# Inverse norms by VectorE alone, spread by products with the identity, and conv operands loaded three to a product

## The chip, the cores and the metric

The kernel runs on one core of one Trainium2 chip. The metric is the device time of one execution in microseconds (us). Engines are named as the profile names them: PE is TensorE (PEld its weight loads), DVE is VectorE, ACT is ScalarE, POOL is GpSimd, SP is SyncE, whose queue here issues nearly all DMA transfers. L217 means line 217 of the kernel.

## What is computed

One layer of a streaming encoder over 1056 tokens (1024 of a prompt, 32 of a sample), model width 1024, all in float32: a sliding-window attention and a gated short convolution side by side, then attention to 256 memory tokens, then an MLP, each behind an RMS norm. Cut to what matters:

```python
def rms_norm(x, g):
    y = x * rsqrt(mean(x * x, axis=-1, keepdims=True) + 1e-6)
    return y * g

h = rms_norm(x, g_mix)
q, k, v, ch, cb, cc, ga, gb = split(h @ w_in)
a = window_attention(q, k, v) @ w_attn_out
conv = causal_depthwise_conv3(cc * ch)
bo = (cb * conv) @ w_conv_out
x = x + (sigmoid(ga) * a + sigmoid(gb) * bo) @ w_mix_out
hc = rms_norm(x, g_cross)
x = x + memory_attention(hc @ w_cq, mem_k, mem_v) @ w_co
hm = rms_norm(x, g_mlp)
x = x + square(relu(hm @ w_up)) @ w_down
y = rms_norm(x, g_final)
```

The keys and values of the memory tokens come from a further RMS norm of the memory input.

## The kernel before

**Layout.** Activations lie transposed: features on the 128 partitions (eight groups of 128, f = 0 to 7), tokens along the free dimension. The tokens are cut into three chunks of 384, 384 and 288 columns (CH). Every float32 product is made of three passes in fp32r: each operand x is split into a rounded part hi (written by ACT) and the rest lo = x - hi (written by DVE), and hi*hi, hi*lo and lo*hi are summed. So a product of a 128-feature output group is 24 matmuls with 24 weights of 128 by 128 (gemm, L183 to L185; the MLP's are at L851 to L853 and L1586 to L1588). A weight of 128 by 1024 is fetched by SP (L145), split by ACT (L125) and DVE (L126), two or three ahead of its use.

**Order.** The work is written as a list of items; a planner with a timeline of its own then orders the instructions of each engine and hands out buffers from pools. Where an instruction is wrapped in pin, it stays in program order with the other pinned ones of its engine. Each engine runs its own instructions in that order, and a waiting instruction holds back all behind it. Scratch tiles named "ct" come from one ring of six buffers (NCT, function tmp). Accumulators in PSUM ("acc") are three until the last stage and six in it.

**Norms.** Most products are made of x times the gain, and their result is multiplied by the inverse norm of its token; for that, and where an operand is normed ahead (L820, L1212), all 128 partitions need the inverse norms as a row, R. chunk_stats does this in two steps. stats_col: squares are summed over feature groups, then per block of 128 tokens a product with a column of ones gives the sum of squares as a column of 128 tokens (pq, L214); DVE scales it and adds the epsilon (L216), ACT takes the square root (L217), DVE the reciprocal (L218) and one Newton step (L219 to L221), which leaves up to three columns in rcol. stats_row: per block the identity is scaled by the column, as hi on ACT (L229) and lo on DVE (L230), into two ct tiles; two products with a matrix of ones (L231, L232) sum each over the partitions and so leave the inverse norms along the free dimension in all partitions (pr), which ACT copies to R (L242) or, for the memory, to mr (L404). stats_col runs 13 times: three times at the start (norm_x), once for the memory, twice for each chunk around the attention to the memory, three times for the final norm. stats_row runs 12 times; the last chunk to be finished, chunk 1, needs columns alone, as it is turned by transposes and leaves token by token (final_last, L1654).

ACT holds one table of functions at a time. Square root, exponential and sigmoid sit in different ones, and a load is seen in the trace (ACT_TABLE_LOAD) where the next function needs another. At the start norm_x takes a dummy square root (L282), so that the first real one finds its table.

**From the gates to the mix.** The gate pairs end the projections of the first stage. close_gates (L865) then lists the conv operands of chunks 1 and 2, eight tiles each, in `wanted`, and starts the first two. A call pump(n) first splits the tiles that the call before had loaded (ACT L781, DVE L782, both pinned) and then issues n more loads (L786), each into a ct tile. Next comes trunk(0): eight conv output products of chunk 0 (do_conv_out, one for each f), then its eight mix products (do_mix). A conv output product loads m1, the gated attention part, into a ct tile (L1026), multiplies the accumulator by the gate into another (DVE, L1030), adds m1 (POOL, L1031, or DVE for the last f) and splits the sum for the mix. Beside its eight conv output products runs the pump, two loads to a product. Small loads of the memory's keys and values (L1056, L1065), with splits of their own (L1068, L1069), are placed in the same stretch by the planner. The mix of chunk 0 needs all eight sums. Trunks 1 and 2 follow, with the attention of the chunk before to the memory set between their products by hand (beside, cross_steps); do_co (L1183 to L1187) ends that attention, do_mix adds x (L1045), and normed_split (L1212 to L1216) prepares the MLP's operands.

The lines behind the pump beside trunk(0):

```python
left = beside([], trunk(0), [(i, lambda: pump(2)) for i in range(NF)])
item(lambda: pump(0))
```

Of the kernel before, what the change touches and what calls it, by code (L numbers as in the profile page):

```python
# [9 lines left out]

F32 = mybir.dt.float32
F32R = mybir.dt.float32r
AF = mybir.ActivationFunctionType
ALU = mybir.AluOpType
AX = mybir.AxisListType
# [3 lines left out]
P = 128  # L19
# [4 lines left out]
NF = 8  # L24
# [14 lines left out]
def hybrid_step(ctx: ExitStack, tc: tile.TileContext, io):  # L39
    nc = tc.nc  # L40
    act, dve, pool_e, pe, sp = nc.scalar, nc.vector, nc.gpsimd, nc.tensor, nc.sync
# [3 lines left out]
    def nm(s):  # L45
        uid[0] += 1
        return f"{s}_{uid[0]}"
# [11 lines left out]
    misc = ctx.enter_context(tc.tile_pool(name="misc", bufs=1))  # L59
# [6 lines left out]
    prm = misc.tile([P, NPARAM], F32, name="prm")  # L66
    ident = misc.tile([P, P], F32, name="ident")
    ones = misc.tile([P, 1], F32, name="ones")
    ones_r = misc.tile([P, P], F32R, name="ones_r")
    nsink = misc.tile([P, 20], F32, name="nsink")  # L70

    def col(j):
# [28 lines left out]
    def tmp(n, dt=F32):  # L101
        return tp.tile([P, n], dt, tag="ct", bufs=NCT, name=nm("ct"))

    def slot(pool, tag, n, dt=F32R, bufs=None):
        return pool.tile([P, n], dt, tag=tag, bufs=bufs, name=nm(tag))
# [8 lines left out]
    def item(fn, *keys):  # L114
        plan.append((fn, keys))
        worder.extend(keys)
# [31 lines left out]
    def issue_w():  # L148
# [3 lines left out]
        key = worder[wpos[0]]  # L152
        hi = wp.tile([P, 1024], F32R, tag="wh", name=nm("wh"))
        lo = wp.tile([P, 1024], F32R, tag="wl", name=nm("wl"))
        if kept.get(key) is not None:
# [52 lines left out]
    def stats_col(accs, blocks, rcol):  # L208

        nb = len(blocks)  # L210
        pq = ps.tile([P, nb], F32, tag="pt", bufs=2, name=nm("pq"))
        for j, b in enumerate(blocks):
            for i, acc in enumerate(accs):
                pe.matmul(pq[:, j : j + 1], acc[:, b : b + P], ones, start=(i == 0), stop=(i == len(accs) - 1))  # L214
        v, s, y, t = (misc.tile([P, nb], F32, tag=x, bufs=2, name=nm(x)) for x in ("st_v", "st_s", "st_y", "st_t"))
        dve.tensor_scalar(v, pq, 1.0 / D, EPS, op0=ALU.mult, op1=ALU.add)  # L216
        act.activation(s, v, AF.Sqrt)  # L217
        dve.reciprocal(y, s)  # L218
        dve.tensor_mul(t, v, y)  # L219
        dve.scalar_tensor_tensor(t, t, -0.5, y, op0=ALU.mult, op1=ALU.mult)  # L220
        dve.scalar_tensor_tensor(rcol, t, 1.5, y, op0=ALU.add, op1=ALU.mult)  # L221

    def stats_row(blocks, n, rcol):

        pr = ps.tile([P, n], F32, tag="pt", bufs=2, name=nm("pr"))
        dh, dl = tmp(n, F32R), tmp(n, F32R)
        for j, b in enumerate(blocks):
            s, r, eye = slice(j * P, b + P), rcol[:, j : j + 1], ident[:, j * P - b :]
            act.mul(dh[:, s], eye, r)  # L229
            dve.scalar_tensor_tensor(dl[:, s], eye, r, dh[:, s].bitcast(F32), op0=ALU.mult, op1=ALU.subtract)  # L230
        pe.matmul(pr, ones_r, dh, start=True, stop=False)  # L231
        pe.matmul(pr, ones_r, dl, start=False, stop=True)  # L232
        return pr

    def chunk_col(c):
# [12 lines left out]
    def square_acc(x, f, c, on_pool=False):  # L248
# [7 lines left out]
        else:  # L256
            act.activation(sq, x, AF.Square)  # L257
        if f:
# [18 lines left out]

    def norm_x():
        pool_e.memset(ones, 1.0)
        act.copy(ones_r, ones.to_broadcast([P, P]))  # L280
        warm = misc.tile([P, 1], F32, name="warm")
        act.activation(warm, ones, AF.Sqrt)  # L282
        make_identity(nc, ident)
        raws = []

        def load_x():
            for c, (o, n) in enumerate(CH):
                raw = raw_tile()[:, : NF * n].rearrange("p (f t) -> p f t", f=NF)
                for h in range(4):
                    sp.dma_start(raw[:, 2 * h : 2 * h + 2], io[f"x{c}"][:, 2 * h : 2 * h + 2])  # L290
                    if c == h == 0:
                        sp.dma_start(prm, io["params"])
                        fetch_w()
                if c == 0:
                    fetch_w()
                    fetch_w()
                raws.append(raw)

        def parts(c, fs, pinned=lambda x: x):
            for f in fs:  # L300
                xg[c][f] = (slot(xpool, f"X{c}", CH[c][1]), slot(xpool, f"X{c}", CH[c][1]))
                scaled_split(*xg[c][f], raws[c][:, f], G_MIX + f, pinned)

        def squares(c):
            n = CH[c][1]
            acc = st.tile([P, n], F32, tag="sum", bufs=2, name=nm("sum"))
            for f in range(NF):
                sq = st.tile([P, n], F32, tag="sq", bufs=2, name=nm("sq")) if f else acc
                (pin if c else lambda x: x)(act.activation(sq, raws[c][:, f], AF.Square))
                if f:  # L310
                    dve.tensor_add(acc, acc, sq)
            accs[c] = [acc]

        with tc.manual_schedule(engines={mybir.EngineType.SP}):
            load_x()
        with tc.manual_schedule(engines={mybir.EngineType.Activation, mybir.EngineType.DVE}):
            parts(0, range(2))
            issue_w()
            parts(0, range(2, NF))
            issue_w()  # L320
            issue_w()
            squares(0)
        wk, wv = ready[0][1], (ready[1][1], ready[2][1])
        kt = at_tile([P, NT], F32, "kt")
        ktt[0] = kt
        vs3 = {}

        def scaled(c):

            o, n = CH[c]  # L330
            chunk_row(c)
            k = kt[:, o : o + n]
            pool_e.tensor_tensor(k, k, R[c], op=ALU.mult)
            for j in range(3):
                v_scale(vs3[c, j], c, j)

        for c, (o, n) in enumerate(CH):
            a = acc_tile([P, n])
            gemm(a, wk, xg[c])
            act.copy(kt[:, o : o + n], a)  # L340
            if c < 2:
                parts(c + 1, range(NF), pin)
            vs3[c, 0] = v_block(wv, c, 0)
            if c:
                scaled(c - 1)
            chunk_col(c)
            vs3[c, 1] = v_block(wv, c, 1)
            vs3[c, 2] = v_block(wv, c, 2)
            if c < 2:
                squares(c + 1)  # L350
            if c == 1:
                mem_load_x()
        for key in start_keys:
            next_w(key)

        def end():
            scaled(2)
            sp.dma_start(io["o_k"][0], kt[:, 896:])
            v = tmp(256)
            sp.dma_start(v, io["cache_v"])  # L360
            vtile(v)
            dve.tensor_scalar_mul(nsink, prm[:, SINK0 : SINK0 + 20], -1.0)

        start_end.extend([(0, end), (2, mem_parts)])
# [10 lines left out]
    def mem_parts():  # L375
        mx = mact.pop()
        his, los = (raw_tile(F32R)[:, : NF * 256].rearrange("p (f t) -> p f t", f=NF) for _ in range(2))
        for f in range(NF):
# [399 lines left out]
    def pump(n):  # L778
        for into, at, t, get in coming:
            hi, lo = into[at] = (get(), get())  # L780
            pin(act.copy(hi, t))  # L781
            pin(dve.tensor_sub(lo, t, hi.bitcast(F32)))  # L782
        coming.clear()
        for into, at, src, cols, get in wanted[:n]:
            t = cols() if callable(cols) else tmp(cols)
            sp.dma_start(t, src)  # L786
            coming.append((into, at, t, get))
        del wanted[:n]
# [684 lines left out]
    def beside(steps, fillers, late=()):  # L1473
        for i, filler in enumerate(fillers):
            item(*filler)
            for x in [x for at, x in late if at == i]:
                item(lambda x=x: x())
            if steps:
                kind, what = steps.pop(0)
                for x in what:  # L1480
                    if kind == "items":
                        item(*x)
                    else:
                        item(lambda x=x: x())
        return steps

    def trunk(c):
        return [(do_conv_out(c, f), ("w_conv_out", f)) for f in range(NF)] + [
            (do_mix(c, f), ("w_mix", f)) for f in range(NF)
        ]  # L1490
# [2 lines left out]
    for name, n in (("w_conv_out", NF), ("w_mix", NF), ("w_cq", 2), ("w_co", 2), ("w_up", NF)):  # L1493
        kept.update(((name, j), None) for j in range(1, n, 2))

    left = beside([], trunk(0), [(i, lambda: pump(2)) for i in range(NF)])
    item(lambda: pump(0))
    left = beside(cross_steps(0), trunk(1))

    normed = lambda c, at: [(at + f, lambda f=f: normed_split(c, f)) for f in range(NF)]  # L1500
    left = beside(left + cross_steps(1), trunk(2), normed(0, 6))
    left = beside(left + cross_steps(2), up0(0) + up0(1), normed(1, 0))
# [337 lines left out]
```

## Time and profile before

| | |
|---|---|
| median of three runs | 1791.7 us |
| lowest and highest run | 1789.65 and 1793.85 us |
| profiled execution, span | 1791.7 us |
| busy: PE, DVE, ACT, POOL | 1754.1, 1173.1, 799.6, 594.2 us |
| moved by DMA | 331.5 MB, mean 185 GB/s |
| mean granted clock of TensorE | 0.994 |

The profile is of one execution on the chip. A row of a group gives line, engine, operation, output and inputs, shapes, count, busy time and mean duration of one, and the idle time of the engine just before them with what ended it. A row in order of time gives start, duration and the instruction, with the wait before it in brackets. Matmuls are pipelined: their durations overlap, and what one costs in a stream is the distance from its start to the next start. A stretch gives the busy time of each engine, the TensorE clock that was granted (1.00 is full speed), the share of time that the DMA engines were busy and what they moved.

### The profile page before, as it was taken

Reading aid. Unit: us, or ns where it says so; the run is one execution under the profiler, and the core shown is the slowest. Engines: PE = TensorE matmul, PEld = TensorE weight load, DVE = VectorE, ACT = ScalarE, POOL = GpSimd, SP = SyncE. Lnnn points to the kernel's source line nnn. Section 1 sums busy time; section 2 is a strip of 40 time slices with the busy share of each in tenths; the row PEclk is TensorE's granted clock in tenths of the full one; section 3 lists DMA queues with packets and bytes.
Section 4 is the critical chain, followed back from the end, with each engine's and each line's share of the span. In section 5 each row is a group of like instructions: output and inputs, shape, how many; then the busy total and the mean of one; then the engine's idle time right before and its main releaser. Section 6 shows DMA issues by size and latency. Waiting matters only on the chain. (4 is left out here: it accounts for less than half of the span.)

```text
span 1791.7 us, 30247 instructions
## 1 busy us (share of the span) xinstructions
PE 1754.1 (98%) x11110; PEld 1732.5 (97%) x11110; DVE 1173.1 (65%) x2165; ACT 799.6 (45%) x1566; POOL 594.2 (33%) x681
## 2 busy tenths in 40 slices
PE   8999999999999999999999989999999999999997
PEld 8999999999999999999999989999999999999997
DVE  6776767868666646546566777767566676436763
ACT  8643534435345334334565745632222343324453
POOL 0013146553453444511224142386554300100111
PEclk9999999999999999999999999999999999999999
DMA  5232234344346888758765657754333487446673
GB/s 181 98 116 92 87 104 153 118 142 144 137 151 239 286 281 282 270 196 274 261 208 201 229 187 252 254 180 148 131 127 137 150 291 246 144 131 214 198 234 125
DMA packets 183858, 331.50 MB, mean 185 GB/s; under 512 B 18768, under 2 KB 139376, under 8 KB 183584
## 3 DMA queue, kind: packets, MB, share of 16 engines
q1 hardware_dynamic: 169936, 281.18, 46.7%
q0 software_dynamic: 13776, 48.41, 7.6%
q8 instruction: 87, 1.43, 0.3%
q14 instruction: 59, 0.48, 0.1%
HBM read 242.99 MB, written 86.52 MB: 184 GB/s over the span
## 5 line engine op out<-in xcount | busy, mean ns | idle before, releaser
L126 DVE TENSOR_TENSOR wl<-wr,wh 128x1024 fp32r<-128x1024 f32 x225 | 300.9, 1337 | 178.6 <-ACT wh L125 175.8
L125 ACT CAST wh<-wr 128x1024 fp32r<-128x1024 f32 x225 | 236.8, 1052 | 401.1 <-PE acc L1587 103.1
L183 PE MATMUL acc<-X,wh 128*128 128x384 f32 (+1 forms) x864 | 282.2, 327 | 8.2 <-ACT wh L125 8.2
L184 PE MATMUL acc<-X,wh 128*128 128x384 f32 (+1 forms) x864 | 279.4, 323 | 0.0
L185 PE MATMUL acc<-X,wl 128*128 128x384 f32 (+1 forms) x864 | 278.9, 323 | 0.3 <-DVE wl L126 0.3
L183 PE MATMUL acc<-Y,wh 128*128 128x384 f32 (+1 forms) x624 | 201.9, 325 | 0.8 <-DVE ct L1242 0.3
L185 PE MATMUL acc<-Y,wl 128*128 128x384 f32 (+1 forms) x624 | 202.1, 324 | 0.0
L184 PE MATMUL acc<-Y,wh 128*128 128x384 f32 (+1 forms) x624 | 201.7, 324 | 0.0
L259 POOL TENSOR_TENSOR xacc<-xacc,ct 128x384 f32<-128x384 f32 (+1 forms) x62 | 75.4, 1218 | 339.8 <-ACT ct L257 334.2
L183 PEld LDWEIGHTS acc<-X,wh 128*128 128x128 f32 x864 | 163.2, 189 | 8.8 <-ACT wh L125 8.2
L184 PEld LDWEIGHTS acc<-X,wh 128*128 128x128 f32 x864 | 163.5, 189 | 0.6
L185 PEld LDWEIGHTS acc<-X,wl 128*128 128x128 f32 x864 | 163.1, 189 | 0.8 <-DVE wl L126 0.8
L183 PEld LDWEIGHTS acc<-Y,wh 128*128 128x128 f32 x624 | 117.4, 189 | 1.8 <-DVE ct L1089 0.6
L185 PEld LDWEIGHTS acc<-Y,wl 128*128 128x128 f32 x624 | 117.8, 189 | 0.0
L184 PEld LDWEIGHTS acc<-Y,wh 128*128 128x128 f32 x624 | 117.7, 189 | 0.0
L1586 PE MATMUL acc<-Y,wh 128*128 128x384 f32 (+1 forms) x352 | 112.7, 322 | 1.1 <-DVE lt L1378 0.7
L1587 PE MATMUL acc<-Y,wh 128*128 128x384 f32 (+1 forms) x352 | 113.1, 321 | 0.0
L1588 PE MATMUL acc<-Y,wl 128*128 128x384 f32 (+1 forms) x352 | 112.8, 321 | 0.0
L125 ACT CAST PTh<-pt 128x512 fp32r<-128x512 f32 (+3 forms) x94 | 46.2, 517 | 115.8 <-PE pt L572 107.8
L707 POOL TENSOR_TENSOR xacc<-xacc 128x256 f32<-128x256 f32 x92 | 83.7, 909 | 4.9
L851 PE MATMUL acc<-Y,wh 128*128 128x384 f32 x248 | 83.1, 336 | 1.8 <-ACT wh L125 1.8
L1244 POOL TENSOR_TENSOR ct<-ct 128x288 f32<-128x288 f32 (+1 forms) x48 | 45.2, 943 | 116.7 <-DVE ct L1240 45.7
(360 smaller groups left out, 4759.5 us busy)
## 6 DMA issues: line engine op xcount, KB each, us to landing
wr<-in_w_in SPq DMA_DIRECT2D x53, 512.0 KB, 3.5
wr<-in_w_up SPq DMA_DIRECT2D x48, 512.0 KB, 4.0
wr<-in_w_down SPq DMA_DIRECT2D x32, 512.0 KB, 4.0
wr<-wsum_d SPq DMA_DIRECT2D x32, 512.0 KB, 3.9
wl<-wl_d SPq DMA_DIRECT2D x28, 512.0 KB, 4.6
wr<-in_w_conv_out SPq DMA_DIRECT2D x24, 512.0 KB, 4.4
wr<-in_w_mix SPq DMA_DIRECT2D x24, 512.0 KB, 4.4
ct<-b_d SPq DMA_DIRECT2D x48, 192.0 KB, 4.1
```

Source lines behind the costliest of these rows:

```text
L125: act.copy(hi, src)
L126: dve.tensor_sub(lo, src, hi.bitcast(F32))
L183: pe.matmul(out, wh[:, a], hi, start=(k == 0), stop=False)
L184: pe.matmul(out, wh[:, a], lo, start=False, stop=False)
L185: pe.matmul(out, wl[:, a], hi, start=False, stop=(k == len(acts) - 1))
L259: pool_e.tensor_tensor(acc, acc, sq, op=ALU.add)
L707: pin(pool_e.tensor_tensor(t[:, to], t[:, x], t[:, y], op=ALU.add))
L851: pe.matmul(acc, wh[:, a], hi, start=(start and k == 0), stop=False, skip_group_check=True)
L1244: pool_e.tensor_tensor(h, t, t, op=ALU.mult)
L1586: pe.matmul(a, wh[:, s], hi, start=(start and k == 0), stop=False, skip_group_check=True)
L1587: pe.matmul(a, wh[:, s], lo, start=False, stop=False, skip_group_check=True)
L1588: pe.matmul(a, wl[:, s], hi, start=False, stop=(stop and k == len(acts) - 1), skip_group_check=True)
```

## The change

Three things. The inverse norm no longer goes through ACT: its first guess comes from integer operations on the bits of the value (a shift to the right by one, then a constant minus the result), followed by three Newton steps in place of one, all on DVE. The column is spread over rows by products: the column is rounded to fp32r as rh, the rest is rl, and for each block of 128 tokens the column, repeated 128 times by its access pattern, is the weight and the identity in fp32r the moving operand; so no scaled identity and no ct tile is needed. The dummy square root at the start and the matrix of ones go, a copy of the identity in fp32r comes. And the pump beside the conv output products of chunk 0 loads three tiles to a product for products 0 to 4, and splits the last of them at product 5.

```diff
-    ones_r = misc.tile([P, P], F32R, name="ones_r")
+    ident_r = misc.tile([P, P], F32R, name="ident_r")
...
-        v, s, y, t = (misc.tile([P, nb], F32, tag=x, bufs=2, name=nm(x)) for x in ("st_v", "st_s", "st_y", "st_t"))
+        v, y, t = (misc.tile([P, nb], F32, tag=x, bufs=2, name=nm(x)) for x in ("st_v", "st_y", "st_t"))
         dve.tensor_scalar(v, pq, 1.0 / D, EPS, op0=ALU.mult, op1=ALU.add)
-        act.activation(s, v, AF.Sqrt)
-        dve.reciprocal(y, s)
-        dve.tensor_mul(t, v, y)
-        dve.scalar_tensor_tensor(t, t, -0.5, y, op0=ALU.mult, op1=ALU.mult)
-        dve.scalar_tensor_tensor(rcol, t, 1.5, y, op0=ALU.add, op1=ALU.mult)
+        dve.tensor_single_scalar(t.bitcast(I32), v.bitcast(I32), 1, op=ALU.arith_shift_right)
+        dve.tensor_scalar(y.bitcast(I32), t.bitcast(I32), -1, 0x5F3759DF, op0=ALU.mult, op1=ALU.add)
+        for to in (y, y, rcol):
+            dve.tensor_mul(t, v, y)
+            dve.scalar_tensor_tensor(t, t, -0.5, y, op0=ALU.mult, op1=ALU.mult)
+            dve.scalar_tensor_tensor(to, t, 1.5, y, op0=ALU.add, op1=ALU.mult)
...
         pr = ps.tile([P, n], F32, tag="pt", bufs=2, name=nm("pr"))
-        dh, dl = tmp(n, F32R), tmp(n, F32R)
+        rh, rl = (misc.tile([P, len(blocks)], F32R, tag=x, bufs=2, name=nm(x)) for x in ("st_h", "st_l"))
+        dve.tensor_copy(rh, rcol)
+        dve.tensor_sub(rl, rcol, rh.bitcast(F32))
         for j, b in enumerate(blocks):
-            s, r, eye = slice(j * P, b + P), rcol[:, j : j + 1], ident[:, j * P - b :]
-            act.mul(dh[:, s], eye, r)
-            dve.scalar_tensor_tensor(dl[:, s], eye, r, dh[:, s].bitcast(F32), op0=ALU.mult, op1=ALU.subtract)
-        pe.matmul(pr, ones_r, dh, start=True, stop=False)
-        pe.matmul(pr, ones_r, dl, start=False, stop=True)
+            s, eye = slice(j * P, b + P), ident_r[:, j * P - b :]
+            for r in (rh, rl):
+                pe.matmul(pr[:, s], r[:, j : j + 1].to_broadcast([P, P]), eye, start=(r is rh), stop=(r is rl))
         return pr
...
         pool_e.memset(ones, 1.0)
-        act.copy(ones_r, ones.to_broadcast([P, P]))
-        warm = misc.tile([P, 1], F32, name="warm")
-        act.activation(warm, ones, AF.Sqrt)
         make_identity(nc, ident)
+        act.copy(ident_r, ident)
...
-    left = beside([], trunk(0), [(i, lambda: pump(2)) for i in range(NF)])
-    item(lambda: pump(0))
+    left = beside([], trunk(0), [(i, lambda i=i: pump(3 if i < 5 else 0)) for i in range(6)])
```

More of the change, by code (lines that the diff above doesn't have):

```diff
@@ L12 @@
 F32R = mybir.dt.float32r
+I32 = mybir.dt.int32
 AF = mybir.ActivationFunctionType
```

## The prediction

> **What bounds the kernel now.** I read the page first, then the busy time in stretches of 20 us, then TensorE's own waits. The page:
>
> ```profile
> span 1791.7 us, 30247 instructions
> PE 1754.1 (98%) x11110; PEld 1732.5 (97%) x11110; DVE 1173.1 (65%) x2165; ACT 799.6 (45%) x1566; POOL 594.2 (33%) x681
> ```
>
> TensorE (PE) is busy for 98% of the span, and no other engine is near that. So a microsecond of products added is, as a rule, a microsecond of time, and a microsecond taken from ScalarE (ACT) or VectorE (DVE) is worth something only where PE stood idle for it. The idle time is 1791.7 - 1754.1 = 37.6 us. The stretches say where (columns: stretch, length, busy time of PE, PEld, DVE, ACT, POOL, then granted clock, DMA share, GB/s):
>
> ```profile
> 680.00:700.00 20.00, 17.09 (x85) 16.30 (x85) 13.14 (x16) 7.05 (x13) 10.10 (x14) 0.83 0.78 264
> 820.00:840.00 20.00, 19.55 (x112) 19.06 (x110) 13.75 (x22) 10.72 (x19) 3.65 (x4) 1.00 0.84 283
> 840.00:860.00 20.00, 18.07 (x99) 17.12 (x100) 15.01 (x26) 11.73 (x22) 4.14 (x3) 1.00 0.75 251
> 1020.00:1040.00 20.00, 15.26 (x97) 13.67 (x96) 16.46 (x28) 12.45 (x23) 6.76 (x6) 0.95 0.73 253
> 1040.00:1060.00 20.00, 18.10 (x103) 17.10 (x103) 15.53 (x22) 10.24 (x18) 13.31 (x13) 0.88 0.49 159
> 1740.00:1760.00 20.00, 19.00 (x106) 17.93 (x106) 10.61 (x15) 11.77 (x20) 4.54 (x4) 1.00 0.64 207
> 1780.00:1800.00 20.00, 3.27 (x31) 3.03 (x29) 2.89 (x8) 3.19 (x6) 0.00 (x0) 0.79 0.22 80
> sum 1800.00, PE 1754.10 PEld 1732.51 DVE 1173.12 ACT 799.59 POOL 594.22; mean PE 19.49 PEld 19.25 DVE 13.03 ACT 8.88 POOL 6.60
> ```
>
> The end, after the last product, holds 11.7 - 3.3 = 8.4 us of it. The largest hole inside is 1020 to 1060 (4.7 + 1.9 = 6.6 us), where attention to the memory of chunk 1 runs beside the mix of chunk 2; then 680 to 700 (2.9 us) and 820 to 860 (0.45 + 1.93 = 2.4 us), the step from the conv output products to the mix of chunk 0. TensorE's waits and the start:
>
> ```profile
> PE acc L183 <- ACT wh L125: 9.8, 2, 8.2
> PE acc L1183 <- DVE Gb L1045: 3.9, 4, 1.5
> 4.19 1.12 ACT L262 ACTIVATE X<-raw,prm 128x384 fp32r<-128x384 f32 x2 [0.35 <-DMA prm<-in_params]
> 7.07 1.05 ACT L125 CAST wh<-wr 128x1024 fp32r<-128x1024 f32 x1 [1.75 <-DMA wr<-in_w_in]
> ```
>
> The 8.2 us are the start. There ACT waits for the parameters at 4.19 and the first weight at 7.07, so a table load and a dummy square root less ahead of 4.19, and a copy of the identity in their place, change nothing: 0. No wait of PE names a line of the norm (L216 to L242).
>
> **The change part by part.** The profiled execution spans 1791.7 us, which is also the median of the runs (1791.7, between 1789.65 and 1793.85), so the sum is made against 1791.7.
>
> *Row products.* Twelve calls spread inverse norms over rows. Each now issues two products of 384, 288 or 256 columns; afterwards six of up to 128 columns (four for the memory), each with a weight of its own.
>
> ```profile
> L231 PEld LDWEIGHTS pr<-ct,ones_r x12: 187/188/192, 36.1 to 1732.2; 128*128 128x128 f32 x12
> L231 PE MATMUL pr<-ct,ones_r x12: 279/331/338, 36.2 to 1732.3; 128*128 128x384 f32 x7, 128*128 128x288 f32 x4, 128*128 128x256 f32 x1
> 95.42 0.27 PE L546 MATMUL sc<-KSh,QA 128*128 128x128 f32 x1
> 95.98 0.28 PE L547 MATMUL sc<-KSl,QA 128*128 128x128 f32 x1
> 1732.35 0.33 PE L231 MATMUL pr<-ct,ones_r 128*128 128x384 f32 x1
> 1732.52 0.34 PE L1587 MATMUL acc<-Y,wh 128*128 128x384 f32 x1
> 785.83 0.29 PE L185 MATMUL pa<-X,wl 128*128 128x288 f32 x1
> 785.96 0.29 PE L183 MATMUL pa<-X,wh 128*128 128x288 f32 x1
> ```
>
> Durations overlap, so the price is from start to start: 0.17 us for 384 columns, 0.13 for 288. For 128 columns in fp32r, 95.42 and 95.98 are the first and the last of six in a row, five steps: 0.56 / 5 = 0.112 us. They don't cost a third of 384. A row of 384 goes from 2 x 0.17 = 0.34 to 6 x 0.112 = 0.67, plus 0.33; of 288 from 0.26 to 0.67, plus 0.41 (its last block has 32 columns, taken at the same price); the memory's from 0.26 (the 288 row) to 0.45, plus 0.19. Sum 7 x 0.33 + 4 x 0.41 + 0.19 = **4.1 us**, on the bounding engine. No row shows a weight that is one column read 128 times. Below: 0, if 128 columns cost a third of 0.17, as 6 x 0.057 = 0.34. Above: the load's 0.188 us uncovered, 6 x 0.188 = 1.13, so 7 x 0.79 + 4 x 0.87 + (0.75 - 0.26) = 9.5. I take 4.1, the row of the same shape.
>
> The Trainium skill's page "TensorE: Matmul & The Clock Gate" (section on LDWEIGHTS) prices a load by its 128 columns at 107 ns, which the 0.112 agrees with; its section "Back-to-back issue gap" gives 81 ns for 128 columns in a stream of such pairs. By that the rows would cost 7 x 0.15 + 4 x 0.23 + 0.06 = 2.0, an estimate from that page, and the whole would come out some 2 us lower.
>
> *ACT and DVE.* Removed: 35 scalings by the identity on each engine, 13 square roots and their table loads, of which ACT holds:
>
> ```profile
> L217 ACT ACT_TABLE_LOAD x4 | 5.1, 1283 | 0.1
> L1125 ACT ACT_TABLE_LOAD x3 | 3.8, 1283 | 0.1
> L229 ACT ACTIVATE ct<-ident,rc 128x128 fp32r<-128x128 f32 (+1 forms) x33 | 10.6, 385 | 1.6 <-DVE rc L221 1.6
> L230 DVE SCALAR_TENSOR_TENSOR ct<-ident,rc,ct x33: 246/346/918, 33.0 to 1732.6; 128x128 fp32r<-128x128 f32 x29, 128x32 fp32r<-128x32 f32 x4
> ```
>
> That is about 10.6 + 5.1 + most of 3.8 = 19 us less on ACT. DVE loses 33 x 0.35 = 12 us and 13 reciprocals and gains, by call, two integer operations and six of Newton (13 x 8 x 0.16 = 17 us) and two small copies a row (24 x 0.16 = 4): about +7. Both lie under PE's products, so 0; without that cover DVE's 7 us would count. Two "ct" buffers of six are no longer held for a row, worth something only where PE waits behind that ring (the second rival).
>
> *The end.* Here nothing hides the norm:
>
> ```profile
> 1782.92 0.16 DVE L216 TENSOR_SCALAR st_v<-pq 128x3 f32<-128x3 f32 x1 [2.92 <-PE pq L214]
> 1783.12 0.20 ACT L217 ACTIVATE st_s<-st_v 128x3 f32<-128x3 f32 x1 [1.91 <-DVE st_v L216]
> 1783.76 0.16 DVE L220 SCALAR_TENSOR_TENSOR st_t<-st_t,st_y 128x3 f32<-128x3 f32 x1
> 1783.96 0.16 DVE L221 SCALAR_TENSOR_TENSOR rc<-st_t,st_y 128x3 f32<-128x3 f32 x1
> ```
>
> Dependent operations on DVE start 0.20 apart. Now the last one starts 1.04 after the first; afterwards it is the eleventh after it, 11 x 0.20 = 2.2. So **+1.2 us**, and the outputs and their stores follow that much later. An integer operation isn't shown; at half or twice 0.20 for the two the term is 1.0 to 1.6.
>
> *Norm of chunk 0 near the end.* Between 1725.94 and 1733.95 its chain stands among other DVE work:
>
> ```profile
> 1725.94 0.15 DVE L216 TENSOR_SCALAR st_v<-pq 128x3 f32<-128x3 f32 x1
> 1733.95 0.48 ACT L242 COPY R<-pr 128x384 f32<-128x384 f32 x1 [0.83 <-PE pr L232]
> ```
>
> 8.0 us. The trip to ACT and the scalings go, nine more DVE operations come, each behind whatever stands there. Outputs of chunk 0 wait for it, and behind these on SP the last operand loads, for which PE is idle 1.0 us at 1740 to 1760. Between -1.0 (that idle gone) and +1.8 (nine at 0.20, none hidden); I take 0.
>
> *Conv operands, three to a product.* After the gates' own two, 14 loads remain; two to a product they end at product 6, three to a product at product 4, and the last splits (L781, L782) come at product 5 rather than after 6. The loads on SP move ahead of weight loads and of m1 (L1026). Now:
>
> ```profile
> 806.97 0.56 DVE L1030 TENSOR_TENSOR ct<-acc,Ga 128x384 f32<-128x384 f32 x1 [1.21 <-PE acc L185]
> 843.51 0.55 DVE L1030 TENSOR_TENSOR ct<-acc,Gb 128x384 f32<-128x384 f32 x1
> 819.59 1.01 POOL L1031 TENSOR_TENSOR ct<-ct,ct 128x384 f32<-128x384 f32 x1 [4.42 <-DVE mkl L126]
> 820.63 0.32 SPq L1026 DMA_DIRECT2D ct<-m_d  x1
> 840.14 0.44 PE L183 MATMUL acc<-M,wh 128*128 128x384 f32 x1 [0.58 <-DVE ct L1030]
> 852.50 0.44 PE L183 MATMUL acc<-M,wh 128*128 128x384 f32 x1 [1.66 <-ACT wh L125]
> 851.09 0.41 ACT L1068 CAST mv<-mvr 128x256 fp32r<-128x256 f32 x1 [1.61 <-DMA mvr<-in_cmem_v]
> ```
>
> DVE takes up a conv product every (843.51 - 806.97) / 7 = 5.2 us, where PE needs 24 x 0.17 = 4.1: a load of m1 is issued when POOL's add of the product before has freed its buffer. DVE ends some 7 us late and PE pays 0.58, then 1.66 behind a load for the memory in ACT's queue. With no operand loads in the last three products that stretch of DMA is lighter. At best all 2.4 us idle of 820 to 860 go; at worst the first five products get slower (third rival). I take **-1.0**: the 0.58 and a quarter of the rest, as the loop through POOL remains.
>
> Sum: 4.1 + 1.2 + 0 - 1.0 = +4.3, so **1796.0 us**, with its own range 1792 to 1800.
>
> **The rivals.**
> *One: the small products hide their weight loads* and the rows cost nothing: 1791.7 + 1.2 - 1.0 = 1791.9. For it, 128 x 0.17 / 384 = 0.057; against it, the run at 0.112.
> *Two, on the other side: faster.* Lighter ACT and two more free buffers let the adds of L1045 come in time and the hole at 1020 to 1060 closes. Its price is 6.6 us idle and what the clock lost there, 20 x (0.05 + 0.12) = 3.4: 1796.0 - 10.0 = 1786.0. It decides once L1183 no longer waits for L1045. For it, the seven table loads of L217 and L1125 fall between 887 and 1154 us, and most go; against it, DVE is the fuller engine there (16.5 of 20) and gains work.
> *Three: three loads starve the ring of six.* A load more is 0.196 MB at 283 GB/s = 0.7 us a product, so 5.9 us against 4.1; after five DVE is 9 us late, more than the two spare accumulators cover (2 x 4.1). PE then waits about 2 us, and an idle time of this kind has cost the clock:
>
> ```profile
> 687.21 0.69 PE L851 MATMUL acc<-X,wh 128*128 128x384 f32 x1 [2.91 <-ACT wh L125]
> ```
>
> In its stretch the clock fell to 0.83, 20 x 0.17 = 3.4 us. Together 1796.0 + 1.0 + 2 + 3.4 = 1802.4.
> *Four: loads of the repeated column don't overlap*: 9.5 for 4.1, 1801.4.
>
> **How the numbers follow.** Forecast 0.44, rivals one 0.12, two 0.24, three 0.14, four 0.06. A measurement of this kernel can tell about 0.2%, 3.6 us, from no change: the bounds are 1788.1 and 1795.3. Faster: rival two but for 0.02, 0.22. Within: one 0.12, 0.02 of two, and 0.16 of the forecast (its range from 1792 up to 1795.3): 0.30. Slower: the remaining 0.28, three and four: 0.48. The range runs from 1786.5 to 1802, leaving out half of two and half of three.
>
> **What would show it.** Row products at 0.11 from start to start, 70 in place of 24; eleven DVE steps of 0.20 at the end; no table load after 900; L1030 every 5 us or so and less idle at 840 to 860. Wrong, if the row products take 0.06 or 0.19, or if idle time between 800 and 1180 moves by more than 4 us either way, since the planner orders everything anew.

## The result and the profile after

| | before | after |
|---|---|---|
| median, four runs each, side by side | 1792.8 us | 1806.3 us |
| lowest and highest run | 1789.65 and 1795.52 us | 1802.1 and 1809.16 us |
| profiled execution, span | 1791.7 us | 1803.8 us |

The changed kernel is slower: the ratio is 1.0081, 95% interval 1.0057 to 1.0106, or 14.5 us with 10 to 19. The forecast was 1796.0 us, and its range ended at 1802. The page of the changed kernel, its first line and its busy times:

```profile
span 1803.8 us, 30353 instructions
PE 1757.3 (97%) x11156; PEld 1737.1 (96%) x11156; DVE 1182.3 (66%) x2245; ACT 776.0 (43%) x1509; POOL 594.7 (33%) x681
```

PE executes 46 more products, ACT is 24 us lighter and DVE 9 us heavier; 19 and 7 were forecast. PE's busy time grew by 3.2 us and its idle time by 8.9 (from 37.6 to 46.5). The same stretches of 20 us say where the idle time is (columns as before):

```profile
680.00:700.00 20.00, 18.25 (x99) 17.49 (x98) 13.90 (x19) 9.23 (x16) 11.22 (x13) 0.91 0.84 295
820.00:840.00 20.00, 13.97 (x70) 13.36 (x68) 11.28 (x18) 7.95 (x15) 2.80 (x2) 0.91 0.80 252
840.00:860.00 20.00, 18.70 (x96) 18.17 (x97) 11.83 (x25) 8.63 (x19) 2.99 (x3) 0.91 0.52 175
1020.00:1040.00 20.00, 19.67 (x147) 19.24 (x147) 18.27 (x38) 14.63 (x29) 5.30 (x5) 1.00 0.66 231
1040.00:1060.00 20.00, 15.56 (x80) 13.39 (x79) 14.96 (x24) 10.46 (x18) 13.36 (x13) 0.91 0.59 193
```

Between 820 and 860 us, where 2.4 us were idle, 7.3 are, and the granted clock, 1.00 there before, is 0.91 in both stretches: 40 x 0.09 = 3.6 us more. That is the stage of the conv output products. The hole at 1020 to 1060 did not close: 4.8 us idle in place of 6.6. Between 680 and 700 the idle time fell from 2.9 to 1.8 us. PE's waits, in order of time, between 818 and 860, and then the rows around the loop of the conv output products (start, duration, instruction; SPq is the issue of a transfer by SP):

```profile
831.02 0.41 PE L184 MATMUL acc<-Y,wh 128*128 128x384 f32 x1 [3.04 <-DVE ct L1030]
841.15 0.41 PE L184 MATMUL acc<-Y,wh 128*128 128x384 f32 x1 [4.15 <-DVE ct L1030]
```

```profile
820.38 0.41 SPq L1026 DMA_DIRECT2D ct<-m_d  x1
...
826.09 1.78 POOL L1031 TENSOR_TENSOR ct<-ct,ct 128x384 f32<-128x384 f32 x1 [8.49 <-DMA mkr<-mk_d]
827.89 0.32 SPq L786 DMA_DIRECT2D ct<-bc_d  x1
...
829.22 0.79 SPq L786 DMA_DIRECT2D ct<-bc_d  x1
830.10 0.42 SPq L1026 DMA_DIRECT2D ct<-m_d  x1
830.33 0.55 DVE L1030 TENSOR_TENSOR ct<-acc,Gb 128x384 f32<-128x384 f32 x1
...
835.30 1.02 POOL L1031 TENSOR_TENSOR ct<-ct,ct 128x384 f32<-128x384 f32 x1 [7.43 <-DMA mkr<-mk_d]
836.34 0.32 SPq L786 DMA_DIRECT2D ct<-bc_d  x1
...
837.92 0.42 SPq L1026 DMA_DIRECT2D ct<-m_d  x1
```

The reader is to follow one turn. POOL's add ends at 835.30 + 1.02 = 836.32 and frees the buffer of m1; at 836.34 SP, which had been waiting for one, issues a conv operand load; the load of m1 stands behind the operand loads in SP's queue and goes out at 837.92; POOL can add only when m1 has landed, 826.09 - 820.38 = 5.7 and 835.30 - 830.10 = 5.2 us after its issue. So everything stands in one ring: add, operand load, m1, add. One turn is the distance of two m1 loads, 9.7 and 7.8 us here, where they were 5.1 to 6.5 us apart before. (The profile names a load for the memory, mk_d, as what released POOL. The add itself reads the product of L1030, done long before, and m1, and SP's waits below agree with m1.) SP's own waits in this stage, between 800 and 862 us, first before, then after (line waited at, by whom it was released, us in total, times, longest):

```profile
SPq L1026 <- POOL ct L1031: 6.7, 7, 1.3
```

```profile
SPq L786 <- POOL ct L1031: 6.5, 5, 2.0
SPq L786 <- DMA ct<-m_d: 6.4, 3, 2.8
```

Before, it was the m1 load itself that waited for the add of an earlier product, 1.3 us at most. Now it is the operand load ahead of it (L786) that waits, and m1 with it. The two rows after are two parts of the same waits: before the load at 827.89, SP waits 2.8 us until m1 has landed and then 2.0 until the add that reads it is done. All these tiles come from the ring of six ct buffers.

The end of the kernel, as forecast, is a chain of twelve operations on DVE (the first, the two integer ones, and the last):

```profile
1794.01 0.16 DVE L217 TENSOR_SCALAR st_v<-pq 128x3 f32<-128x3 f32 x1 [2.92 <-PE pq L215]
1794.20 0.17 DVE L218 TENSOR_SCALAR st_t<-st_v 128x3 int32<-128x3 int32 x1
1794.40 0.17 DVE L219 TENSOR_SCALAR st_y<-st_t 128x3 int32<-128x3 int32 x1
...
1796.18 0.16 DVE L223 SCALAR_TENSOR_TENSOR rc<-st_t,st_y 128x3 f32<-128x3 f32 x1
```

The last starts 2.17 us after the first, before it was 1.04: +1.13. The row products stand 0.11 us apart:

```profile
44.03 0.28 PE L234 MATMUL pr<-ident_r,st_l 128*128 128x128 f32 x1
...
44.48 0.27 PE L234 MATMUL pr<-ident_r,st_l 128*128 128x128 f32 x1
```

These are the second and the last of the six of one row: (44.48 - 44.03) / 4 = 0.112 us, the distance of the rows of that shape before. (The first stands at 43.97, only 0.06 us ahead, so the six take some 0.62 us and not 0.67.) The repeated column as a weight costs nothing extra.

### The profile page after: what moved, and what is told of

It reads as the page before. It is cut to its first block, busy times and chain, and to the rows that moved or that the text cites. A ratio compares the mean times of both kernels' runs of the same rounds, so it can differ in the third digit from the quotient of the medians.

```text
span 1803.8 us, 30353 instructions
## 1 busy us (share of the span) xinstructions
PE 1757.3 (97%) x11156; PEld 1737.1 (96%) x11156; DVE 1182.3 (66%) x2245; ACT 776.0 (43%) x1509; POOL 594.7 (33%) x681
## 5 line engine op out<-in xcount | busy, mean ns | idle before, releaser
L853 PE MATMUL acc<-Y,wl 128*128 128x384 f32 x248 | 83.8, 338 | 0.0
```

Of the source, the lines that this page charges most:

```text
L853: pe.matmul(acc, wl[:, a], hi, start=False, stop=(k == 3), skip_group_check=True)
```

## The experiments

The first theory (P) after the result was that most of the loss comes from the three loads to a product; its rival (N) that the norms, and the new order that the planner made of them, cost most. All runs of a group share the runs of the kernel before on the same chip, 27 to 31 each with a median of 1792.1 to 1792.6 us; the three groups ran on three chips, so kernels of different groups are compared by their ratios. Times below are the ratio's distance from 1, times 1792 us, with the 95% interval.

**One part alone.** Four kernels.

e1: the three loads alone.

```diff
-    left = beside([], trunk(0), [(i, lambda: pump(2)) for i in range(NF)])
-    item(lambda: pump(0))
+    left = beside([], trunk(0), [(i, lambda i=i: pump(3 if i < 5 else 0)) for i in range(6)])
```

> The kernel before with three conv operand loads to a product as the only edit; the norms stay. Theory P (the three loads starve the ring of six ct buffers, and most of the loss comes from there): VectorE takes up the first five conv products some 8.4 us apart, as in the changed kernel, TensorE waits about 7 us for L1030, the granted clock falls to about 0.9 in two stretches of 20 us, and the time is 6 to 9 us over the kernel before. Theory N (the norms and the new order that the planner makes of them cost most): L1030 still 5 to 6 us apart, within 3 us of the kernel before.

e2: the changed kernel with those lines as before, so both parts of the norm alone.

> The changed kernel with two conv operand loads to a product again: both parts of the norm and nothing else. Theory P: the row products (+4.1) and the end (+1.2) are left, 4 to 6 us over the kernel before, and L1030 about 5.2 us apart again. Theory N: 10 us or more over the kernel before, as the changed kernel.

e3: the kernel before with the new stats_row (row products with the identity), square root and Newton step as before.

> The kernel before with the spreading over rows by products with the identity alone; square root on ScalarE and two loads to a product stay. If the row products cost what their start to start says: 46 more of 0.11 less the width saved, +4.1 us. If small products hide their weight loads: 0 to +1. If leaving the ct ring earlier is worth something: under 0. If the new order of the planner costs by itself: above +6.

e4: the kernel before with the new stats_col (integer guess, three Newton steps, no square root), the scaled identity as before.

> The kernel before with the inverse norm by VectorE alone; the scaled identity and two loads to a product stay. If only the end feels it: +1.2 us, with the final norm's chain 2.2 us long. If the longer chains delay R of the chunks in the middle too, as at 1092 us in the changed kernel (2.5 us idle): +3 to +6. If the table loads were worth something: under 0.

| | median | over the kernel before |
|---|---|---|
| e1, three loads alone | 1800.4 us | +7.7 us (5.0 to 10.4) |
| e2, both parts of the norm | 1796.9 us | +4.1 us (2.0 to 6.5) |
| e3, row products alone | 1796.4 us | +3.6 us (0.9 to 6.3) |
| e4, inverse norm on DVE alone | 1796.8 us | +3.9 us (1.8 to 6.3) |

Theory P holds: e1 and e2 together make 11.8 us of the 14.5, within the errors the whole, and in e2 L1030 is 5.2 us apart again. PE's waits in e1, from the view that lists them by releaser, and its two stretches:

```profile
PE acc L183 <- DVE ct L1030: 7.4, 2, 4.2
```

```profile
820.00:840.00 20.00, 12.62 (x61) 12.04 (x60) 10.59 (x17) 7.39 (x14) 3.13 (x3) 0.90 0.80 259
840.00:860.00 20.00, 20.00 (x108) 20.00 (x108) 12.75 (x24) 10.25 (x21) 3.73 (x4) 0.93 0.57 180
```

7.4 us idle in place of 2.4, and a clock of 0.90 and 0.93, that is 20 x (0.10 + 0.07) = 3.4 us: 5.0 + 3.4 = 8.4, measured 7.7. VectorE's steps at L1030 were near the 8.4 us expected:

```profile
810.86 0.55 DVE L1030 TENSOR_TENSOR ct<-acc,Ga 128x384 f32<-128x384 f32 x1
819.39 0.54 DVE L1030 TENSOR_TENSOR ct<-acc,Ga 128x384 f32<-128x384 f32 x1
828.49 0.55 DVE L1030 TENSOR_TENSOR ct<-acc,Gb 128x384 f32<-128x384 f32 x1
838.71 0.55 DVE L1030 TENSOR_TENSOR ct<-acc,Gb 128x384 f32<-128x384 f32 x1
```

8.5, 9.1 and 10.2 us apart. In e4 the expectation of +1.2 for the end alone lies outside the interval, and e3 and e4 do not add up to e2 (7.5 against 4.1, which the intervals still allow). So the inverse norm on DVE needed a run of its own, e10.

**Buffer or bandwidth, and the price of a row product.** Which part of the loop makes it slow? The prediction's third rival had priced it as transfer time. The rival theory (R) is the ring: the three tiles that were loaded and wait for their split, m1 and the product of accumulator and gate are five of six buffers. The product can be written over the gate, which nobody reads again. That takes one buffer a product out of the ring and leaves all transfers as they are.

```diff
             a = acc_tile([P, n])
             gemm(a, w, bcp[c])
-            t = tmp(n)
-            dve.tensor_mul(t, a, sg[c][f])
+            t = sg[c][f]
+            dve.tensor_mul(t, a, t)
```

e5 is e1 with this edit, e6 the kernel before with it.

> As e1 (three loads to a product, norms of before), but the product of accumulator and gate is written over the gate, so that a conv output product takes one ct buffer in place of two. Theory R (what starves is the ring of six: three loaded tiles, m1 and the product fill five of it, so loads wait for the adds on GpSimd, and m1 waits behind them in SP's queue): L1030 about 5 us apart again, TensorE's wait for L1030 under 2 us in place of 7.4, and the time within 3 us of the kernel before. Theory D (the third rival as it was written: three loads take 0.7 us of DMA more to a product): L1030 still 6 us or more apart, 5 to 8 us over the kernel before.

> The kernel before with the product of accumulator and gate written over the gate, two loads to a product. Theory R: the ring was already the limit in the kernel before (L1030 5.2 us apart where TensorE needs 4.1), so the steps come to 4.1 to 4.6 us, part of the 2.4 us idle between 820 and 860 goes, 0 to 3 us faster. Theory D: no change, 5.2 us apart.

e8 spreads the loads thinner instead of denser:

```diff
-    left = beside([], trunk(0), [(i, lambda: pump(2)) for i in range(NF)])
-    item(lambda: pump(0))
+    left = beside([], trunk(0), [(i, lambda i=i: pump(2 if i < 3 else 1 if i < 11 else 0)) for i in range(12)])
```

> The kernel before with the 14 conv operand loads spread the other way: two to a product for three products, then one to a product up to the third mix product. Theory R: fewer buffers of the ring are held at a time, so L1030 comes nearer to 4.1 us apart from the fourth product on, and the time is 0 to 3 us under the kernel before. If a load a product is hidden anyway and the idle time of 840 to 860 comes from the memory's loads: no change within 2 us.

e7 is e2 with each pair of row products issued three times:

```diff
-            for r in (rh, rl):
-                pe.matmul(pr[:, s], r[:, j : j + 1].to_broadcast([P, P]), eye, start=(r is rh), stop=(r is rl))
+            for _ in range(3):
+                for r in (rh, rl):
+                    pe.matmul(pr[:, s], r[:, j : j + 1].to_broadcast([P, P]), eye, start=(r is rh), stop=(r is rl))
```

> As e2 (both parts of the norm, two loads to a product), but every pair of row products is issued three times over, the last pair standing: 140 products of up to 128 columns more. At 0.112 us from start to start each they cost 15.7 us over e2 (1812 or so); if small products hide their weight loads, 0.057 each and 8 us (1805); if the load of a repeated column is not overlapped, 0.188 each and 26 us (1823).

| | median | over the kernel before |
|---|---|---|
| e5, three loads, product over the gate | 1793.0 us | +1.1 us (-1.1 to 3.2) |
| e6, two loads, product over the gate | 1790.1 us | -0.9 us (-3.4 to 1.6) |
| e8, loads spread thinner | 1789.2 us | -2.5 us (-4.8 to -0.2) |
| e7, row products thrice | 1813.5 us | +22.4 us (20.1 to 24.7) |

e5 decides for the ring: the same three loads, the same bytes, and the loss of 7.7 us is down to 1.1, with 0 in the interval. The first two stretches of e5's stage and its first and last step at L1030:

```profile
800.00:820.00 20.00, 20.00 (x117) 20.00 (x116) 12.91 (x19) 8.56 (x14) 2.13 (x2) 1.00 0.93 322
820.00:840.00 20.00, 19.42 (x111) 19.10 (x110) 13.66 (x22) 10.38 (x20) 3.04 (x3) 1.00 0.90 294
```

```profile
805.30 0.56 DVE L1030 TENSOR_TENSOR Ga<-acc,Ga 128x384 f32<-128x384 f32 x1 [1.29 <-PE acc L185]
...
838.98 0.55 DVE L1030 TENSOR_TENSOR Gb<-acc,Gb 128x384 f32<-128x384 f32 x1
```

The DMA engines move 322 GB/s where the changed kernel, short of buffers, has 252 in its stalled stretch, so bandwidth was not what held the steps at 8.4 us. With the DMA engines busy for 0.93 and 0.90 of e5's two stretches there is little of it to spare, though. The eight steps stand (838.98 - 805.30) / 7 = 4.8 us apart, and no wait of PE names L1030 any more. What remains in e5 is a wait of 3.3 us behind a load for the memory in ACT's queue, which the kernel before also has (1.66 us), and with it a clock of 0.91, where it was 1.00 before:

```profile
851.63 0.41 PE L183 MATMUL acc<-M,wh 128*128 128x384 f32 x1 [3.27 <-ACT wh L125]
840.00:860.00 20.00, 16.36 (x81) 15.11 (x80) 13.63 (x22) 9.62 (x19) 4.57 (x4) 0.91 0.60 190
```

So between 820 and 860 e5's profile still has 4.2 us idle where the kernel before has 2.4; it is of the slowest of e5's twelve runs, 1798.2 us against a median of 1793.0.

In e6 the stage between 800 and 880 is full in all four stretches and L1030 steps every 4.6 us; its gain of 0.9 us is within its interval, so the theory's "0 to 3 faster" is neither shown nor refuted by the time. e8 agrees in another way, 2.5 us faster with an interval that just excludes 0: fewer buffers are held at a time, L1030 is 4.6 us apart from the fourth product on, and PE is busy for 39.90 of the 40 us that had 2.4 idle.

e7 prices the row product: e7 less e2 is 1792 x (1.0125 - 1.0023) = 18.3 us, with some 3 us of uncertainty, for 140 products: 0.131, between 0.108 and 0.154. Hidden loads (0.057) and exposed ones (0.188) are excluded. It is a little over the 15.7 us that the rows 0.112 apart give; R also comes 1.3 us later in each row of three blocks, which may be the rest; that was not shown.

**The chain on DVE, and the two edits together.** e10 is e4 with six Newton steps for three, which doubles what was suspected.

```diff
-        for to in (y, y, rcol):
+        for to in (y, y, y, y, y, rcol):
```

> As e4 (inverse norm by VectorE alone, scaled identity, two loads to a product), with six Newton steps in place of three in all thirteen calls: nine dependent operations of 0.20 us more in each. If only the last call is on the path: 1.8 us over e4. If the calls in the middle of the kernel are too (R of the chunks comes later, products wait for it): 5 us or more over e4.

e9 is e8 with the product over the gate, e11 the changed kernel's norms with the loads spread as in e8, and e12 has one load to a product:

```diff
-    left = beside([], trunk(0), [(i, lambda: pump(2)) for i in range(NF)])
-    item(lambda: pump(0))
+    left = beside([], trunk(0), [(i, lambda i=i: pump(1 if i < 14 else 0)) for i in range(15)])
```

> The kernel before with both of what took pressure off the ring: loads spread as in e8 and the product written over the gate as in e6. If each removes a cost of its own: 2 to 5 us under the kernel before. If both remove the same 2.4 us of idle time between 820 and 860: about as e8, 2.5 us under it.

> The changed kernel's norms with the loads spread as in e8 instead of three to a product. If the two edits add: e2's +4 and e8's -2.5 to -3, so about 1.5 us over the kernel before; if the norms' cost hangs on the loads: 4 us or more over it, as e2.

> The kernel before with one conv operand load to a product, from the first conv output product to the sixth mix product. If a load to a product costs a buffer of the ring and with it time at L1030: steps of 4.1 to 4.5 us from the first product on, as fast as e8 or faster, 2 to 5 us under the kernel before. If the operands of chunk 1 then come too late or the mix products' own loads meet them: over e8.

| | median | over the kernel before |
|---|---|---|
| e10, six Newton steps | 1809.3 us | +16.7 us (13.4 to 19.7) |
| e9, spread and product over the gate | 1790.3 us | -2.7 us (-4.7 to -0.5) |
| e11, new norms, loads spread | 1794.5 us | +1.4 us (-0.7 to 3.6) |
| e12, one load to a product | 1788.3 us | -3.4 us (-5.7 to -1.1) |

e10 is 12.7 us over e4, uncertain by some 4, where the end accounts for 1.8: the chains in the middle cost time too. PE's waits in e10, in order of time, show two places, the row of the memory and a row of the attention to the memory; a stretch beside them shows the first in its busy time:

```profile
92.44 0.39 PE L233 MATMUL pr<-ct,ones_r 128*128 128x256 f32 x1 [0.54 <-ACT ct L231]
97.53 0.40 PE L184 MATMUL acc<-X,wh 128*128 128x288 f32 x1 [0.40 <-DVE ct L407]
...
1080.71 0.61 PE L233 MATMUL pr<-ct,ones_r 128*128 128x288 f32 x1 [3.88 <-ACT ct L231]
```

```profile
80.00:100.00 20.00, 17.97 (x118) 17.04 (x119) 13.93 (x38) 7.02 (x10) 2.54 (x6) 1.00 0.45 154
```

Before, 80 to 100 was busy throughout and no product with the ones waited; in e4 the stretch is busy too, and the row that waits 3.88 at 1080 here waits 1.9 us. So of the 12.7 us the end makes 1.8, the stretch 2.0 (half of it behind the chain, half behind DVE's splits of weights at 80 and 83) and the row 2.0. The rest was not located, and the planner's new order may have a part in it. In the changed kernel, with three steps, PE stands idle behind the second of these rows too (L1089 multiplies an accumulator by R, and the next product waits for that accumulator), and the chain on DVE ahead of it shows why:

```profile
1092.45 0.44 PE L184 MATMUL acc<-Y,wh 128*128 128x384 f32 x1 [2.50 <-DVE ct L1089]
```

```profile
1078.04 0.16 DVE L217 TENSOR_SCALAR st_v<-pq 128x3 f32<-128x3 f32 x1 [4.60 <-PE pq L215]
...
1080.30 0.33 DVE L219 TENSOR_SCALAR st_y<-st_t 128x3 int32<-128x3 int32 x1
1080.55 1.21 DVE L127 TENSOR_TENSOR wl<-wr,wh 128x1024 fp32r<-128x1024 f32 x1
1081.68 1.18 DVE L1216 TENSOR_TENSOR Y<-ct,Y 128x384 fp32r<-128x384 f32 x1
1082.78 0.60 DVE L1212 SCALAR_TENSOR_TENSOR ct<-Ga,prm,R 128x384 f32<-128x384 f32 x1
1083.31 0.15 DVE L221 TENSOR_TENSOR st_t<-st_v,st_y 128x3 f32<-128x3 f32 x1
...
1086.69 0.16 DVE L223 SCALAR_TENSOR_TENSOR rc<-st_t,st_y 128x3 f32<-128x3 f32 x1
```

Between steps of 0.16 us stand operations of 0.6 to 1.2 us of other work, in the planner's order, so the chain takes 8.65 us from first start to last and not 2.17; before, the chain at this place took 4.97 (from 1071.01 to 1075.98) and PE's wait for L1089 was 0.29 us. e9 and e8 are alike, which fits both edits taking away one and the same idle time. e11 shows that the loss of the loads can be undone under the new norms too, and agrees with the two edits adding (+1.4, where e2 and e8 give +1.6). e12 has the lowest ratio of the study, 0.19% under the kernel before (0.9981, 0.9968 to 0.9994); the intervals of e8 and e9 overlap with it, so it is not shown to be faster than those. Its L1030 is 4.6 us apart. Its PE is busy without a gap between 820 and 860:

```profile
820.00:840.00 20.00, 20.00 (x117) 20.00 (x116) 14.35 (x24) 9.83 (x18) 6.54 (x4) 1.00 0.89 302
840.00:860.00 20.00, 20.00 (x117) 20.00 (x116) 16.66 (x23) 13.25 (x24) 4.26 (x4) 1.00 0.83 285
```

The gains of e8, e9 and e12 are what is left over: their profiles have 4.1 to 5.6 us idle between 1480 and 1780, where the kernel before has 1.3. What brings that was not followed.

## Why the prediction was wrong

The direction was right, by the two terms of the norm; the size was not, 1796.0 us forecast and 1806.3 measured, since the term of the loads had the wrong sign.

**Conv operands, three to a product: the step that failed.** The prediction took -1.0 here ("the 0.58 and a quarter of the rest, as the loop through POOL remains"). Alone it costs +7.7 us. The prediction saw the loop, that a load of m1 is issued when POOL's add has freed its buffer, and quoted the steps of 5.2 us. For its term it looked at the end of the stage, where loads are fewer, and left the first five products to the third rival. It did not count what a third load does to the ring: five of six buffers held, so the operand loads themselves wait for the add, and m1, behind them in one queue, waits with them. A step of the loop then holds the whole landing time of m1, 5.2 to 5.7 us, on top of the add (1.0 to 1.8) and the issues (2.2 from 827.89 to 830.10, 1.6 from 836.34 to 837.92).

**The third rival came true, at another price.** It had the place and the ring, PE's wait and the clock. The clock loss of 3.4 us came out (3.6 in the changed kernel, 3.4 in e1), in part by luck: it was taken from one wait of 2.9 us and 0.83 in one stretch, and it came from two waits of 3 to 4 us and 0.90 to 0.93 in two. But it worked out the step as transfer time, 0.7 us more to a load at 283 GB/s, which gave 5.9 us a step and 2 us of waiting (its own figures, 9 us late less 8.2 covered, give 0.8). Measured were steps of 8.4 us, (840.45 - 806.83) / 4 by the first and the fifth start at L1030, and 7.2 us of waiting. e5 shows that the bytes did not set that step: with the same bytes it is 4.8. With the measured wait and clock the rival's sum is 1796.0 + 1.0 + 7.2 + 3.6 = 1807.8.

**Row products** were right: 0.112 from start to start in the trace, 0.131 with an uncertainty of 0.023 by tripling, +3.6 us (0.9 to 6.3) by the time of e3, which holds the rest of that edit too, where 4.1 stood. The first and the fourth rival fall with that. The Trainium skill's page "TensorE: Matmul & The Clock Gate" (section "Back-to-back issue gap") states 81 ns for 128 columns; by that the 140 products of e7 would cost 11.3 us, an estimate from that page, below the 15 to 21 us measured, so the measurement decides against it here.

**The end** was right, +1.13 for +1.2, integer operations included (0.20 apart like the others).

**The norm of chunk 0 near the end**, taken as 0: the chain grew from 8.0 to 11.6 us (1735.46 to 1747.06), the 1.0 us idle at 1740 to 1760 is gone, and 0.4 is new at 1720 to 1740. No run isolates it.

**ACT and DVE, costed at 0:** the loads on ACT went (13 table loads became 5, one of them at 909 us, so "no table load after 900" was wrong by one), and no gain in time is seen from it. On DVE the cover is thin in the middle: nine operations more in each call cost e10 12.7 us. What the three steps of the change itself cost outside the end could not be measured well. e4 says 3.9 - 1.1 = 2.8 us, e2 less e3 says 4.1 - 3.6 - 1.1 = -0.6, each uncertain by about 3.

**The second rival** came in small part: L1183's wait for L1045 fell from 3.9 to 1.3 us, and the hole at 1020 to 1060 from 6.6 us to 4.8, but 2.5 us are new at 1092. In e2, with the same norms, the hole has 6.4 us, so the gain is not shown to come from the norms; idle time there moves between neighbours from kernel to kernel. Between 800 and 1180, where the prediction called 4 us either way a sign of being wrong, the idle time went from 13.7 to 18.6 us, nearly all of it between 820 and 860.

| term | forecast | measured |
|---|---|---|
| row products | +4.1 | e3: +3.6 (0.9 to 6.3) |
| the end | +1.2 | trace: +1.13 |
| both parts of the norm | +5.3 | e2: +4.1 (2.0 to 6.5) |
| three loads to a product | -1.0 | e1: +7.7 (5.0 to 10.4) |
| all | +4.3 | +14.5 (10 to 19) |

## What to carry to other kernels

Before loads are moved closer together, count the buffers of the ring they come from, and look at who frees them: when a load waits for a buffer that only a later consumer frees, all loads behind it in the same queue wait too, and the price of a step is then the landing time of the next load, as here, and not its bytes over the bandwidth. The sign in the profile is a wait of the issuing queue for a computing engine inside the loop; here it was 1.3 us at most before, which was the warning. Where a result can be written over an operand that is done, one buffer less a product undid the loss (+1.1 us, -1.1 to 3.2, in place of +7.7).

## What was not expected of the hardware and the schedule

Nine small operations on 3 columns, 0.16 us each, cost 12.7 us in thirteen calls though DVE is busy for two thirds of the time. An engine with spare time was no cover for a chain that is waited for: a step can stand behind a longer operation of other work, as in the rows at 1080. Two stalls of 3 to 4 us, ten us apart, cost half as much again in clock (3.4 to 3.6 us), 0.90 to 0.93 for the 40 us around them. e5, with one wait of 0.6 us there, kept 1.00 up to 840 us, and its one wait of 3.3 us at 851 went with 0.91 for 20 us; the kernel before, with 1.66 us at the same place, kept 1.00. Whether m1 on a queue of its own would have sufficed, with the ring as it is, was not tried.
